# A hybrid decoder layer on one core: order in the head, one PSUM bank, one tie, tiles of their own, and the order of VectorE work in the down product

## The chip, the cores and the metric

The kernel runs on 1 core of one Trainium2 chip. Its time is device microseconds of that core; three runs of the kernel before gave 1724.09, 1722.09 and 1722.20 us, a median of 1722.2 us. The engines are called as in the profile: PE is TensorE (matmuls, and PEld its weight loads), DVE is VectorE, ACT is ScalarE, POOL is GpSimd, SP is the queue that issues the DMAs.

## What is computed

One decoder layer over 16 meta tokens and 1024 real tokens, all in float32. The reference, cut to its stages:

```
xn   = rms_norm(h, mix_pre_g)
proj = xn @ w_in                  # columns z, xbc (x, B, C), dt, q, k, v
y_ssd = ssd_mixer(z, silu(causal_dwconv(xbc)), softplus(dt + bias), ...)   # chunks of 128, a scan over chunks
y_sb  = rms_norm(stick_breaking_attention(q, k, v), sb_norm_g)             # 16 heads of 64
h = h + rms_norm(concat[y_ssd, y_sb] @ w_out, mix_post_g)
xn = rms_norm(h, ffn_pre_g)
gu = xn @ w_up                    # 1024 x 5632
g  = causal_dwconv3(gu[:, :2816])
f  = (gelu(g) * gu[:, 2816:]) @ w_down
h  = h + rms_norm(f, ffn_post_g)
```

## The kernel before

**Products.** Every large float32 product is made of three matmuls on operands split into a high and a low part: high by high, high by low, low by high. The high part is a copy on ACT, the low part a subtraction on DVE or POOL that reads the operand and the high part. Up and down products go through seven Strassen-Winograd products each instead of eight.

**Who orders the instructions.** A planner orders each engine's instructions by its own estimate of the times, except inside blocks in which the order of the text is kept: the head (all engines), the attention (PE alone), and from the second tile of the last mixing projection to the end (PE, DVE, ACT, POOL). `tc.issue_after(i)` ties the instructions traced in its block behind instruction `i` on `i`'s engine. Semaphores are set by a tracker of which instruction reads and writes which part of which tile.

**Head (lines 231 to 348).** Nine row tiles i = 0 to 8 are normed (`norm`, DVE), turned by PE transposes (`turn_x`, L288) and split into `xs`. Into that loop go half chains of the projections of B and C: `project_steps(..., halves_=True)` yields after the first four of eight row blocks of 128, 12 matmuls each. `chains[0]` is B0 and `chains[1]` C0; their weights are split by `split_hi` (ACT) and `split_lo` (POOL, in two halves).

**`to_tokens` (lines 482 to 492)** turns B, C and x back to tokens in three parts, each through a bank of PSUM from `psum_tp`, of which there are two, and copies each part out on DVE.

**Attention (lines 1012 to 1085).** For a pair of heads p and a query tile i, `block_weights` makes the logits z, ACT makes two sigmoids of each chunk (`kp`, `bt`), DVE scans, POOL multiplies; two blocks later `block_turn` transposes `bt` (`tw`) into the same two PSUM buffers (`zz`) that z uses, and ACT copies the result out (`th`; the last such copy is `copied[0]`); `block_mix` is the product with v. In p = 6 and 7 the eight rows of the first half of W_out are brought in by `wout_steps` (lines 898 to 907), here called k0 to k7: a load into one of two buffers `wraw`, a scaled copy on ACT (L904), a subtraction on DVE (L905), which frees the buffer. `STAGE` says after which block how many rows have been traced: k4 after (6,6), k5 after (6,7), k6 after (7,0), k7 after (7,1). Only k4 is tied behind `copied[0]` (line 1060).

**FFN operands (lines 1157 to 1258).** `half_x` makes the operands b11, b21, b22, t1, t2, t3, t4, each as high and low. The high and low tiles of these are flat, 2176 numbers a partition (two of them 2056), and a stretch of 2056 at a fixed offset (`FOFF`, 0 to 48) is seen as 4 x 514. The unsplit ones xa to xd are tiles of 4 x 514. `turn_x2`, `split_x` and `split_b22` fill column ranges of them in pieces: `split_x("t1", 0, 258)` the first columns, `turn_x2(7)` and `turn_x2(8)` the next two lots of 128, `split_b22` columns 2 to 257 and then 0 and 1. `g0_first`, `u0.first_half` and so on are the first products (L1351); each half ends with a copy on ACT (L1357, L1360), and the next product adds to the same bank.

**Down product (lines 1640 to 1880).** 77 steps s of 12 matmuls, in groups of 11 (`DOWN`: n = 1, 2, 6, 5, 3, 7, 4), into banks A or B. In step s come, in this order: the matmuls of s; after the last step of n = 5 and n = 7 the bank's copies or sums out (`evac2`, L1757); loads; `split_step(s + 3)`: ACT high parts (L1670) and DVE low parts (L1671) into one of WB = 3 buffers whi and wlo, which step s has just freed; for n = 6 also a difference `t2` first (L1668); the weight sums of `W_SUMS[s]` (DVE, L1675); one entry of `todo`. The last three steps 74 to 76 are run bank by bank with the end of the layer between.

```
for k in range(NPR):
    for at, args in ((18 + k, ("b11", "b12", "b11", ALU.subtract)), (16 + 2 * k, ("b21", "b21", "b22", ALU.subtract)),
                     (37 + k, ("b12", "b22", "b12", ALU.subtract)), (41 + k, ("b21", "b21", "b11", ALU.add))):
        W_SUMS.setdefault(at, []).append((k, *args))
```

Of the kernel before, what the change touches and what calls it, by code (L numbers as in the profile page):

```python
# [9 lines left out]
F32 = mybir.dt.float32  # L10
F32R = mybir.dt.float32r
BF16 = mybir.dt.bfloat16
AF = mybir.ActivationFunctionType
ALU = mybir.AluOpType
# [43 lines left out]
def tile_layer(ctx: ExitStack, tc: tile.TileContext, x, meta, rows, parts,  # L58
# [115 lines left out]
    def run(steps, n=None):  # L174
        for _ in steps if n is None else zip(range(n), steps):
            pass
# [54 lines left out]
    with tc.tile_pool(name="pre", bufs=3, side="right") as pre, \  # L231
            tc.manual_schedule(engines={ET.PE, ET.Activation, ET.DVE, ET.Pool, ET.SP}):
        spans = [(0, NM)] + [(NM + i * P, P) for i in range(NT)]
        xts = []

        def load_x(i):
            xts.append(pre.tile([P, D], F32, tag="xt", name=f"xt{i}", bufs=9))
            nc.sync.dma_start(out=xts[i][:spans[i][1]], in_=meta if i == 0 else x[(i - 1) * P:i * P, :])

        def raw_of(name, src):  # L240
            raw = wp.tile([P, KB, P], F32, tag="wraw", name=f"wr_{name}")
            nc.sync.dma_start(out=raw, in_=src)
            return raw

        load_x(0)
        load_x(1)
        gpre = row_bcast(pre, 0, D, "gpre")
        load_x(2)
        load_x(3)
        load_x(4)  # L250
        raw_dt = wp.tile([P, KB, 16], F32, tag="wraw", name="wr_dt")
        nc.sync.dma_start(out=raw_dt, in_=w_dt)
        raws = {"B0": raw_of("B0", w_xbc[8])}
        for i in range(5, NT + 1):
            load_x(i)
        raws["C0"] = raw_of("C0", w_xbc[10])
        nc.sync.dma_start(out=pp, in_=parts)

        sums, roots, norms = {}, {}, {}

        def square(i):
            if i <= NT:
                nr = spans[i][1]
                junk = pre.tile([P, D], F32, tag="junk", name=f"junk{i}", bufs=2)
                sums[i] = pre.tile([P, 1], F32, tag="ss", name=f"ss{i}")
                nc.scalar.activation(junk[:nr], xts[i][:nr], AF.Square, scale=D ** -0.5, accum_out=sums[i][:nr])

        def root(i):
            if i <= NT:
                roots[i] = rstd_of(pre, sums[i][:spans[i][1]], 1, spans[i][1], f"pre{i}")  # L270

        def norm(i):
            if i <= NT:
                nr = spans[i][1]
                norms[i] = pre.tile([P, D], F32, tag="xn", name=f"xn{i}", bufs=2)
                nc.vector.scalar_tensor_tensor(norms[i][:nr], xts[i][:nr], roots[i][:nr], gpre[:nr],
                                               op0=ALU.mult, op1=ALU.mult)

        def turn_x(i):
            c0, nr = spans[i]  # L280
            tps = []
            for hf in range(2):
                tp = (psum_tp, psum_z, psum_sd)[(2 * i + hf) % 3](f"xtp{i}_{hf}")
                if (2 * i + hf) % 3:
                    tp = tp.rearrange("p (a b) -> p a b", b=P)
                for b in range(4):
                    k = 4 * hf + b
                    nc.tensor.transpose(tp[:, b, :nr], norms[i][:nr, k * P:(k + 1) * P], ident[:nr, :nr])  # L288
                base = max(a for a, _ in CH if a <= c0)
                h, l = (xs[base][:, j, 4 * hf:4 * hf + 4, c0 - base:c0 - base + nr] for j in range(2))  # L290
                tps.append((tp, h, l))
            for tp, h, _ in tps:
                nc.scalar.activation(h, tp[:, :, :nr], AF.Copy)
            for tp, h, l in tps:
                nc.vector.tensor_tensor(l, tp[:, :, :nr], h.bitcast(F32), op=ALU.subtract)

        ws = {}

        def split_hi(name):
            hi = wp.tile([P, KB, P], F32R, tag="whi", name=f"wh_{name}", bufs=WB)  # L300
            lo = wp.tile([P, KB, P], F32R, tag="wlo", name=f"wl_{name}", bufs=WB)
            nc.scalar.activation(hi, raws[name], AF.Copy)
            ws[name] = hi, lo

        def split_lo(name, part):
            ks = slice(4 * part, 4 * part + 4)
            nc.gpsimd.tensor_tensor(ws[name][1][:, ks], raws[name][:, ks], ws[name][0][:, ks].bitcast(F32),
                                    op=ALU.subtract)

        chains = []  # L310
        for i in range(3):
            square(i)
            root(i)
        norm(0)
        norm(1)
        for i in range(NT + 1):
            if i == 4:
                run(dt_chain, 1)
            if i not in (2, 3):
                norm(i + 2)  # L320
            turn_x(i)
            if i != 2:
                square(i + 2 if i == 3 else i + 3)
                root(i + 2 if i == 3 else i + 3)
            if i == 3:
                norm(4)
                norm(5)
            if i == 1:
                hl = wp.tile([P, KB, 32], F32R, tag="whi", name="wh_dt", bufs=WB)
                nc.scalar.activation(hl[:, :, 0:16], raw_dt, AF.Copy)  # L330
                nc.gpsimd.tensor_tensor(hl[:, :, 16:32], raw_dt, hl[:, :, 0:16].bitcast(F32), op=ALU.subtract)
                dt_chain = dt_steps(hl)
            if i in (3, 4):
                split_hi("B0" if i == 3 else "C0")
            if i in (3, 4, 5):
                split_lo("B0" if i < 4 else "C0", int(i == 5))
            if i == 3:
                square(6)
                root(6)
                split_lo("B0", 1)  # L340
            if i == 3:
                chains.append(conv_chain(8, "B0", ws["B0"], True))
            if i in (5, 6):
                run(chains[0][1], 1)
            if i == 6:
                chains.append(conv_chain(10, "C0", ws["C0"], True))
            if i in (7, 8):
                run(chains[1][1], 1)

    halves = (slice(0, 64), slice(64, 128))  # L350
    M0 = NM - 2
# [111 lines left out]
    with tc.tile_pool(name="ssd", bufs=1, side="right") as sp:  # L463
# [17 lines left out]

        def to_tokens(src, dst, nm):
            for part in range(3):
                tp = psum_tp(f"tt_{nm}_{part}")
                if part == 0:
                    nc.tensor.transpose(tp[:NM, 0, :], src[:, 0:NM], ident)
                    nc.vector.tensor_copy(dst[:NM, 0, :], tp[:NM, 0, :])
                else:
                    for b in range(4):
                        t = 4 * (part - 1) + b  # L490
                        nc.tensor.transpose(tp[:, b, :], src[:, NM + t * P:NM + (t + 1) * P], ident)
                    nc.vector.tensor_copy(dst[:, 1 + 4 * (part - 1):5 + 4 * (part - 1), :], tp)
# [522 lines left out]
    for p in range(8):  # L1015
        for i in range(NT):
# [40 lines left out]
                edge = edge_turn(p - 1)  # L1057
            for _ in range(2):
                if wsteps and len(wres) < min(8, 3 * left[0], STAGE.get((p, i), 0)):
                    with tc.issue_after(copied[0]) if (p, i) == (6, 6) else ExitStack():  # L1060
                        run(wsteps, 1)
            if wsteps and first is None and len(wres) == 8:
                run(wsteps)
# [94 lines left out]
    def half_x(pool, dt, name):  # L1158
        if dt is F32:
            return pool.tile([P, 4, HW], dt, name=name, tag=name)  # L1160
        n, o = (4 * HW, 0) if name in ("b22l", "t1l") else (HF, FOFF.get(name[:-1], 0))
        return pool.tile([P, n], dt, name=name, tag=name)[:, o:o + 4 * HW].rearrange("p (k c) -> p k c", c=HW)

    rt = {n: (half_x(bp, F32R, f"{n}h"), half_x(bp, F32R, f"{n}l")) for n in ("b11", "b21")}
    xa, xb, xc, xd = (half_x(qp, F32, n) for n in ("xa", "xb", "xc", "xd"))
# [494 lines left out]

    def split_step(s):
        n, a, b, p = steps2[s]
        hi = wp.tile([P, 2, 512], F32R, tag="whi", name=f"dh{s}", bufs=WB)
        lo = wp.tile([P, 2, 512], F32R, tag="wlo", name=f"dl{s}", bufs=WB)
        sub = nc.vector.tensor_tensor
        if n == 6:
            wd["t2", p] = db.tile([P, 512], F32, tag="t2", name=f"t2_{p}", bufs=2)
# [8 lines left out]

    W_SUMS = {}
    for k in range(NPR):
        for at, args in ((18 + k, ("b11", "b12", "b11", ALU.subtract)), (16 + 2 * k, ("b21", "b21", "b22", ALU.subtract)),
                         (37 + k, ("b12", "b22", "b12", ALU.subtract)), (41 + k, ("b21", "b21", "b11", ALU.add))):  # L1680
            W_SUMS.setdefault(at, []).append((k, *args))

    for i in range(2, NFF):
# [114 lines left out]
             + [(None, nm, p) for p in range(NPR) for nm in ("b22", "b12")])  # L1798
    last_u = probs[-1]
    n2 = len(steps2)  # L1800
    todo = []
    db, facc = None, {}
    for k in range(3):
# [3 lines left out]
    for s in range(n2):  # L1807
        n, a, b, p = steps2[s]
        if s > 2 and s < n2 - 3:
            down_mm(s, (3, 0, 1, 2))  # L1810
            if p == NPR - 1 and n in (5, 7):
                for t in (3, 0, 1, 2):
                    evac2(n, t, banks[BANK[n], t])
        elif s == n2 - 3:
            for act in todo:
                act()
# [24 lines left out]
                fetch_w(pool or db, (nm,), k)  # L1841
        if s + 4 < n2:
            fetch_a(s + 4)
        if s + 3 < n2:
            split_step(s + 3)
        for args in W_SUMS.get(s, ()):
            w_sum(*args)
# [80 lines left out]
```

## Time and profile before

| | |
|---|---|
| median of 3 runs | 1722.2 us |
| the profiled execution's own time | 1724.05 us |
| its span, first to last instruction | 1722.1 us |
| mean granted TensorE clock | 0.999 |
| busy: PE, DVE, ACT, POOL | 99%, 64%, 48%, 48% of the span |
| moved by DMA | 173.87 MB, 101 GB/s |

A row of the timeline gives the start in us from the span's start, the time taken, engine, line, operation, the tiles written and read, the shapes, and how many such instructions were put together; in brackets stands how long the engine sat idle before it and whose end released it. A row of the windows gives a stretch, its length, the busy time and count of each engine, the granted clock, the share of the DMA engines and GB/s. Matmuls overlap, so a matmul's pace is read from start to start.

### The profile page before, as it was taken

How to read it: one execution, taken by the hardware profiler on the slowest of the kernel's cores; microseconds unless marked ns; L12 is line 12 of the kernel's file. 1: busy time of each engine (PE TensorE's matmuls, PEld its weight loads, DVE VectorE, ACT ScalarE, POOL GpSimd, SP SyncE). 2: the span in 40 equal slices, each digit the busy share in tenths (PEclk: the TensorE clock that was granted, in tenths of full speed). 3: DMA queues.
4: the chain of work that ended last, by engine and by line, in shares of the span. 5: the costliest groups of instructions: out<-in, count | busy, mean ns of one | idle time of the engine just before them, and what ended most of it. 6: DMA issues, size and time to landing. Idle time of an engine off the chain costs nothing. (4 is left out here: it accounts for less than half of the span.)

```text
span 1722.1 us, 28048 instructions
## 1 busy us (share of the span) xinstructions
PE 1699.6 (99%) x11230; PEld 1495.4 (87%) x11230; DVE 1105.8 (64%) x1234; ACT 821.0 (48%) x1370; POOL 833.9 (48%) x641
## 2 busy tenths in 40 slices
PE   7999999999999999999999999999999999999998
PEld 6999889888989998998788788999988888887886
DVE  6752973875676677577530667675666666659777
ACT  5423663554566566557653344433333333344544
POOL 4323664585566575565552222587767777300001
PEclk9999999999999999999999999999999999999999
DMA  4232333231011111112214553233322223395345
GB/s 164 56 114 93 109 124 111 68 104 38 26 38 38 33 31 38 38 50 76 76 66 153 208 172 123 68 111 110 105 92 92 92 92 103 122 327 177 105 115 177
DMA packets 90674, 173.87 MB, mean 101 GB/s; under 512 B 10704, under 2 KB 35816, under 8 KB 90544
## 3 DMA queue, kind: packets, MB, share of 16 engines
q1 hardware_dynamic: 90544, 172.08, 31.3%
q8 instruction: 88, 1.44, 0.3%
q14 instruction: 42, 0.34, 0.1%
HBM read 122.32 MB, written 49.73 MB: 100 GB/s over the span
## 5 line engine op out<-in xcount | busy, mean ns | idle before, releaser
L792 POOL TENSOR_TENSOR bt<-bt,kp 128x256 f32<-128x256 f32 (+7 forms) x128 | 212.0, 1675 | 184.5 <-DVE kp L790 143.6
L790 DVE TENSOR_TENSOR_SCAN kp<-kp,hold 128x272 f32<-128x272 f32 (+7 forms) x128 | 183.4, 1473 | 24.6 <-ACT kp L783 14.3
L1287 POOL TENSOR_TENSOR wlo<-wr,whi 128x1024 fp32r<-128x1024 f32 x43 | 99.3, 2318 | 42.7 <-ACT whi L1286 42.7
L1785 POOL TENSOR_TENSOR fms<-fms 128x1 f32<-128x1 f32 x8 | 2.9, 362 | 223.7 <-ACT dh L1670 197.0
L783 ACT ACTIVATE kp<-z 128x288 f32<-128x288 f32 (+6 forms) x112 | 82.7, 739 | 50.8 <-PE z L782 25.8
L1286 ACT ACTIVATE whi<-wr 128x1024 fp32r<-128x1024 f32 x43 | 45.7, 1064 | 111.2 <-PE fX L1337 67.5
L169 PE MATMUL pj_v<-xs,wh_v 128*128 128x400 f32 (+2 forms) x384 | 95.0, 334 | 0.0
L169 PE MATMUL pj_k<-xs,wh_k 128*128 128x400 f32 (+2 forms) x384 | 94.6, 333 | 0.0
L169 PE MATMUL pj_q<-xs,wh_q 128*128 128x386 f32 (+2 forms) x384 | 93.9, 331 | 0.0
L806 ACT ACTIVATE th<-tw 128x1024 f32<-128x1024 f32 (+2 forms) x96 | 75.5, 815 | 37.5 <-PE tw L804 37.3
L1670 ACT ACTIVATE dh<-ar 128x512 fp32r<-128x512 f32 x77 | 48.5, 630 | 93.2 <-PE dnB L1748 44.7
L169 PE MATMUL pj_X<-xs,wh_X 128*128 128x400 f32 (+2 forms) x384 | 92.0, 327 | 0.0
L169 PE MATMUL pj_z<-xs,wh_z 128*128 128x386 f32 (+2 forms) x384 | 91.6, 326 | 0.0
L1409 DVE SCALAR_TENSOR_TENSOR ga<-gr,pp,ga 128x1024 f32<-128x1024 f32 x44 | 69.0, 1567 | 34.4 <-ACT ga L1402 33.6
L758 DVE CAST qh<-q 128x128 fp32r<-128x128 f32 x64 | 46.5, 727 | 69.1 <-PE z L782 68.7
L976 PE MATMUL mo<-woa,yh 128*128 128x512 f32 x256 | 85.5, 400 | 0.0
L1671 DVE TENSOR_TENSOR dl<-ar,dh 128x512 fp32r<-128x512 f32 x77 | 53.2, 691 | 50.2 <-ACT dh L1670 50.1
L784 ACT ACTIVATE bt<-z 128x288 f32<-128x288 f32 (+6 forms) x112 | 83.1, 742 | 0.0
L804 PE MATMUL tw<-ident,bt 128*128 128x128 f32 x576 | 75.7, 274 | 2.2 <-POOL cb L793 1.7
L819 PE MATMUL av<-th,v 128*64 128x128 f32 x1152 | 77.2, 278 | 0.0
L819 PEld LDWEIGHTS av<-th,v 128*64 128x64 f32 x1152 | 61.6, 137 | 13.8 <-issue 10.9
L804 PEld LDWEIGHTS tw<-ident,bt 128*128 128x128 f32 x576 | 65.4, 141 | 8.7 <-issue 3.1
(560 smaller groups left out, 5603.9 us busy)
## 6 DMA issues: line engine op xcount, KB each, us to landing
wr<-in_w_up SPq DMA_DIRECT2D x44, 512.0 KB
fds<-ga SPq DMA_DIRECT2D x44, 256.0 KB
b<-in_w_down SPq DMA_DIRECT2D x44, 256.0 KB
ar<-fds SPq DMA_DIRECT2D x44, 256.0 KB
fda<-ga SPq DMA_DIRECT2D x33, 256.0 KB
ar<-fda SPq DMA_DIRECT2D x33, 256.0 KB
yk<-yd SPq DMA_DIRECT2D x16, 512.0 KB
wor<-in_w_out SPq DMA_DIRECT2D x12, 512.0 KB
```

The source lines that it names most:

```text
L169: mm(acc[:ncol, :n - s], a[:, k, :ncol], xs[c0][:, b, k, s:n], start=(k == 0 and j == 0), stop=(k == KB - 1 and j == 2))
L783: nc.scalar.activation(kp[:, :, a:a + w], z[:, :, :w], AF.Sigmoid, scale=-QSCALE)
L784: nc.scalar.activation(bt[:, :, a:a + w], z[:, :, :w], AF.Sigmoid, scale=QSCALE)
L790: nc.vector.tensor_tensor_scan(kp[:, j][:, ::-1], kp[:, j][:, ::-1], hold[:, L - n:L][:, ::-1], 0.0, op0=ALU.mult, op1=ALU.max)
L792: nc.gpsimd.tensor_tensor(bt[:, j, 0:m], bt[:, j, 0:m], kp[:, j, 1:m + 1], op=ALU.mult)
L804: nc.tensor.transpose(tw[:, j, b, :], bt[:, j, c0:c0 + P], ident)
L806: copied[0] = nc.scalar.activation(th[:, :, :nb, :], tw[:, :, :nb, :], AF.Copy).ins
L819: mm(av[halves[j], :], v[:, kb, halves[j]], th[:, j, b, :], start=kb == 0, stop=kb == i)
L976: recent[0] = mm(acc, u[:, k, :], v[:, cs], start=(k == 0 and j == 0), stop=(k == 7 and j == 2))
L1287: nc.gpsimd.tensor_tensor(l, raw, h.bitcast(F32), op=ALU.subtract)
L1409: nc.vector.scalar_tensor_tensor(v, self.g[jj][:, :, i:i + 256], fconv_w[:, j, i:i + 1], v, op0=ALU.mult, op1=ALU.add)
L1671: sub(lo[:, k], raw, hi[:, k].bitcast(F32), op=ALU.subtract)
```

## The change

1. Head: the half chains of B0 move from the end of turns i = 5 and 6 to a place before `turn_x(i)` of the same i; those of C0 likewise for i = 7 and 8. C0's chain is opened at i = 7 instead of at the end of i = 6.
2. `to_tokens`: part 0 of B1 goes through a bank of `psum_z` instead of `psum_tp`.
3. W_out's row k5, traced at (6,7), is tied behind `copied[0]` as k4 is.
4. `half_x`: the stretch of 4 x 514 becomes a tile of that shape; what stood ahead of it and behind it in the flat tile becomes two tiles that nothing uses.
5. Down: the sums b21 - b22 of k = 2 to 10 move from steps 20, 22 ... 36 to steps 34 to 42; the sums b21 + b11 from steps 41 to 51 to steps 44 to 54; the split of step 67 is issued in step 65 behind the `evac2` of n = 7 instead of in step 64; the split of the last step, 76, gets buffers of its own.

```
@@ head, in the loop over i
             if i not in (2, 3):
                 norm(i + 2)
+            if i in (5, 6):
+                run(chains[0][1], 1)
+            if i == 7:
+                chains.append(conv_chain(10, "C0", ws["C0"], True))
+            if i in (7, 8):
+                run(chains[1][1], 1)
             turn_x(i)
...
             if i == 3:
                 chains.append(conv_chain(8, "B0", ws["B0"], True))
-            if i in (5, 6):
-                run(chains[0][1], 1)
-            if i == 6:
-                chains.append(conv_chain(10, "C0", ws["C0"], True))
-            if i in (7, 8):
-                run(chains[1][1], 1)
@@ to_tokens
-                tp = psum_tp(f"tt_{nm}_{part}")
+                if part == 0 and nm == "B1":
+                    tp = psum_z(f"tt_{nm}_{part}").rearrange("p (a b) -> p a b", b=P)
+                else:
+                    tp = psum_tp(f"tt_{nm}_{part}")
@@ rows of W_out
-                    with tc.issue_after(copied[0]) if (p, i) == (6, 6) else ExitStack():
+                    with tc.issue_after(copied[0]) if (p, i) in ((6, 6), (6, 7)) else ExitStack():
                         run(wsteps, 1)
@@ half_x
         n, o = (4 * HW, 0) if name in ("b22l", "t1l") else (HF, FOFF.get(name[:-1], 0))
-        return pool.tile([P, n], dt, name=name, tag=name)[:, o:o + 4 * HW].rearrange("p (k c) -> p k c", c=HW)
+        if o:
+            pool.tile([P, o], F32, name=f"{name}o", tag=f"{name}o")
+        t = pool.tile([P, 4, HW], dt, name=name, tag=name)
+        if n > o + 4 * HW:
+            pool.tile([P, n - o - 4 * HW], F32, name=f"{name}e", tag=f"{name}e")
+        return t
@@ split_step
-        hi = wp.tile([P, 2, 512], F32R, tag="whi", name=f"dh{s}", bufs=WB)
-        lo = wp.tile([P, 2, 512], F32R, tag="wlo", name=f"dl{s}", bufs=WB)
+        own = s == len(steps2) - 1
+        hi, lo = ((db if own else wp).tile([P, 2, 512], F32R, tag=f"w{e}" + "l" * own, name=f"d{e[0]}{s}",
+                                           bufs=1 if own else WB) for e in ("hi", "lo"))
@@ W_SUMS
-(16 + 2 * k, ("b21", "b21", "b22", ALU.subtract))
+(16 + 2 * k if k < 2 else 32 + k, ("b21", "b21", "b22", ALU.subtract))
-(41 + k, ("b21", "b21", "b11", ALU.add))
+(44 + k, ("b21", "b21", "b11", ALU.add))
@@ the loop over s
+    LATE = 6 * NPR - 2
...
                 for t in (3, 0, 1, 2):
                     evac2(n, t, banks[BANK[n], t])
+            if s == LATE + 1:
+                split_step(LATE + 3)
...
-        if s + 3 < n2:
+        if s + 3 < n2 and s != LATE:
             split_step(s + 3)
```

More of the change, by code (lines that the diff above doesn't have):

```diff
@@ L1678, in tile_layer @@
     for k in range(NPR):
-        for at, args in ((18 + k, ("b11", "b12", "b11", ALU.subtract)), (16 + 2 * k, ("b21", "b21", "b22", ALU.subtract)),
-                         (37 + k, ("b12", "b22", "b12", ALU.subtract)), (41 + k, ("b21", "b21", "b11", ALU.add))):
+        for at, args in ((18 + k, ("b11", "b12", "b11", ALU.subtract)), (16 + 2 * k if k < 2 else 32 + k, ("b21", "b21", "b22", ALU.subtract)),
+                         (37 + k, ("b12", "b22", "b12", ALU.subtract)), (44 + k, ("b21", "b21", "b11", ALU.add))):
             W_SUMS.setdefault(at, []).append((k, *args))
```

## The prediction

> **What bounds the kernel now.** I read the page first, then a table of stretches, then PE's timeline at each place where PE stands still.
>
> ```profile
> span 1722.1 us, 28048 instructions
> PE 1699.6 (99%) x11230; PEld 1495.4 (87%) x11230; DVE 1105.8 (64%) x1234; ACT 821.0 (48%) x1370; POOL 833.9 (48%) x641
> ```
> ```profile
> 800.00:815.00 15.00, 12.78 (x124) 11.16 (x123) 12.92 (x10) 12.93 (x20) 8.61 (x4) 1.00 0.23 71
> 1060.00:1080.00 20.00, 17.91 (x113) 16.14 (x112) 13.99 (x18) 8.50 (x16) 2.71 (x4) 0.91 0.34 106
> 1500.00:1700.00 200.00, 199.97 (x875) 163.24 (x874) 149.82 (x239) 95.59 (x177) 5.39 (x8) 1.00 0.60 192
> ```
>
> PE is the bound: 1722.1 - 1699.6 = 22.5 us of it are idle, and the change removes no matmul. It can gain only where PE idles, where PE is busy at less than its pace, or where the clock is down; it can lose where it opens a new gap. The table has 2.2 us idle at 800 to 815, 2.1 us at 1060 to 1080 with the clock at 0.91, and none in the down product from 1500, where lost time has to be looked for in the pace.
>
> **The change part by part**
>
> **1. Head.**
>
> ```profile
> 20.99 1.06 PE L288 MATMUL xtp<-ident,xn 128*128 128x128 f32 x8 [1.15 <-DVE xn L276]
> 24.08 1.04 PE L288 MATMUL xtp<-ident,xn 128*128 128x128 f32 x8
> 27.15 1.04 PE L288 MATMUL xtp<-ident,xn 128*128 128x128 f32 x8
> ```
> ```profile
> 17.74 2.02 POOL L307 TENSOR_TENSOR wl_B<-wr_B,wh_B 128x512 fp32r<-128x512 f32 x1
> 21.54 1.29 POOL L307 TENSOR_TENSOR wl_B<-wr_B,wh_B 128x512 fp32r<-128x512 f32 x1
> 24.61 1.29 POOL L307 TENSOR_TENSOR wl_C<-wr_C,wh_C 128x512 fp32r<-128x512 f32 x1
> ```
>
> PE waits 1.15 us for turn 5's normed rows, with B0's first half chain behind it. That chain's low weights are there at 17.74 + 2.02 = 19.76, when PE falls idle (20.99 - 1.15 = 19.84). A turn and a half chain take 27.15 - 24.08 = 3.07 us, so a half chain about 2.0 to 2.3. Ahead of turn 5 it fills the gap and turn 5 begins near 22.1. The second half chain then comes near 23.1 (weights at 22.83), C0's first near 26.2 (weights at 25.90). The margins are 0.1 to 0.3 us. Gain 1.15; with a weight late by its margin 0.8, and no less than 0, since all that is late here was late before.
>
> **2. B1's first part.**
>
> ```profile
> 310.92 0.66 PE L491 MATMUL tt_B<-ident,bt 128*128 128x128 f32 x4 [0.48 <-DVE bn L487]
> ```
>
> Part 2 waits for a bank that part 0 still holds; with part 0 in another bank it does not. Gain 0.48. If the scan's first product wanted that bank next it would be 0.
>
> **3. Row k5.**
>
> ```profile
> 804.62 1.15 ACT L904 ACTIVATE woa<-wor,pp 128x1024 fp32r<-128x1024 f32 x1 [1.99 <-DMA wor<-in_w_out]
> 807.69 0.93 ACT L784 ACTIVATE bt<-z 128x912 f32<-128x912 f32 x1
> 811.45 1.21 ACT L904 ACTIVATE woa<-wor,pp 128x1024 fp32r<-128x1024 f32 x1
> ```
> ```profile
> 808.72 1.06 PE L804 MATMUL tw<-ident,bt 128*128 128x128 f32 x8 [1.69 <-POOL cb L793]
> 810.32 0.44 PE L804 MATMUL tw<-ident,bt 128*128 128x128 f32 x2 [0.53 <-ACT bt L784]
> 838.07 0.48 PE L976 MATMUL mo<-woa,yh 128*128 128x512 f32 x1
> ```
> ```profile
> 829.28 1.28 DVE L905 SCALAR_TENSOR_TENSOR woa<-wor,pp,woa 128x1024 fp32r<-128x1024 f32 x1
> ```
>
> The row at 804.62 cannot be k4, which is tied behind the copies out of this block's transposes (PE begins them at 808.72); k4 is the one at 811.45. So the planner put k5 ahead of k4, and ACT, in order, stood 1.99 us for k5's load and 1.15 us on it with the sigmoids queued behind. The first pair ends at 807.69 + 0.93 = 808.62, and at 808.72 the transposes get that buffer; POOL's product is named, but the end that fits is ACT's. With k5 tied at (6,7), ACT does the sigmoids some 3.1 us earlier, more than the 1.69 + 0.53 = 2.22 that PE idles. Gain 2.22.
>
> What is late next: k5 frees its buffer a block later, so k7's load is issued later; behind it in SP's queue stand the loads of y. PE wants rows k4 to k7 at 838.07, and the last of them was ready at 829.28 + 1.28 = 830.56, so 7.5 us are there, against a block of about 7 to 8 us less what k6 may do first. Bounds: the 2.22 in full, or the same idle anew where ACT waits for another row's load (0), or 1.99 once more on top (-2).
>
> **4. FFN operands.**
>
> ```profile
> 1065.75 0.21 ACT L1248 ACTIVATE b22h<-b22e 128x8 fp32r<-128x8 f32 x1 [4.73 <-DVE b22l L1249]
> 1070.94 0.63 ACT L1242 ACTIVATE t1h<-xa 128x512 fp32r<-128x512 f32 x1 [2.01 <-DVE t1l L1243]
> 1071.47 0.58 ACT L1357 ACTIVATE gr<-g0a 128x516 f32<-128x516 f32 x1
> 1077.16 1.08 ACT L1224 ACTIVATE xb<-x2tp 128x512 f32<-128x512 f32 x2
> ```
> ```profile
> 1068.48 1.29 DVE L1194 SCALAR_TENSOR_TENSOR oxn<-mb,rs_ff,gffn 128x1024 f32<-128x1024 f32 x1 [1.31 <-POOL rs_ff L196]
> 1078.39 0.68 DVE L1226 TENSOR_TENSOR xb<-x2tp,xb 128x512 f32<-128x512 f32 x1
> ```
> ```profile
> 1069.91 1.06 PE L1200 MATMUL x2tp<-ident,oxn 128*128 128x128 f32 x8 [0.96 <-DVE oxn L1194]
> 1072.11 0.58 PE L1351 MATMUL g0a<-b21h,whi2g 128*128 128x258 f32 x1 [1.14 <-ACT gr L1357]
> ```
> ```profile
> 1072.10:1075.20 3.10, 3.09 (x14) 3.09 (x15) 2.17 (x4) 1.56 (x3) 0.00 (x0) 0.50 0.17 67
> ```
>
> Both ACT waits are for DVE to finish reading columns that ACT does not write: columns 0 and 1 of b22h against 2 to 257, a later 128 of t1h against its first 258. In the tiles of 4 x 514 this does not happen: ACT writes xb for turn 7 and turn 8 in one go at 1077.16 while DVE reads turn 7's part only at 1078.39. So I take it that the tracker sees a flat tile's column stretches as one run, and that tiles of that shape lose both waits. Then b22h's edge comes 4.7 us earlier, and turn 8's normed rows (1068.48) wait only for their row sum, some 1.7 us earlier, which covers PE's 0.96; and the copy `gr` (1071.47) no longer stands behind the 2.01 us wait, which covers the 1.14. What PE needs next, t1's last part, moves up with turn 8.
>
> The clock stands at 0.50 for the 3.10 us right behind these gaps: 1.55 us of work lost. With the idle gone I take it as gone. Gain 0.96 + 1.14 + 1.55 = 3.65; bounds 0 (the waits stay) and 3.65. [...]
>
> **5. Down.**
>
> ```profile
> 1533.51 29.92 PE dnB L1748 x132
> 1563.42 22.28 PE dnA L1748 x96
> 1585.71 9.34 PE dnA L1748 x36
> ```
> ```profile
> 1569.01 1.29 DVE L1675 TENSOR_TENSOR b<-b,b 128x512 f32<-128x512 f32 x2
> 1684.01 2.48 DVE L1757 TENSOR_TENSOR facc<-dnA,facc 128x512 f32<-128x512 f32 x4
> ```
> ```profile
> 1684.42 0.39 PE L1748 MATMUL dnA<-dl,dh 128*128 128x512 f32 x1
> 1684.84 0.47 PE L1748 MATMUL dnA<-dh 128*128 128x512 f32 x1
> ```
> ```profile
> 1706.92 0.63 ACT L1670 ACTIVATE dh<-ar 128x512 fp32r<-128x512 f32 x1 [0.95 <-PE dnA L1748]
> ```
> ```profile
> 1707.86 0.39 PE L1748 MATMUL dnA<-dl,dh 128*128 128x512 f32 x1
> 1709.27 0.39 PE L1748 MATMUL dnA<-dh 128*128 128x512 f32 x1
> ```
>
> The pace is 29.92 / 132 = 0.227 us, 2.72 a step. The 132 matmuls of n = 6 take 1595.05 - 1563.42 = 31.63, so 1.71 are lost while PE looks busy. DVE is why: a step there has a difference, two low parts and a sum, 4 x 0.62 = 2.5 us, and 3.1 with a second sum or a bank's sum. In turn over 11 steps: four bank sums and some six second sums are 10 x 0.62 = 6.2 us over a slack of 11 x 0.2 plus the two to three microseconds by which splits run ahead. Without the second sums 2.5 us stay over, which that covers: gain 1.71. The sums land in steps of n = 5 and 3, where there is no difference to make: at most 4 x 0.62 = 2.5 of 2.72. If they did not fit, about 0.2 a step over nine steps would come back, 1.8.
>
> At 1684.42 the pace breaks by 0.42 - 0.23 = 0.19, because the four bank sums wait on DVE behind the split of step 67; moved ahead of it, that and the 0.13 in the next step go: 0.32. The split of 67 is then done near 1687, just as PE comes to it. At 1706.92 the last split has waited for step 73 to free its buffer; four matmuls take 1.41 instead of 0.91. With its own buffer it starts about 1 us earlier: gain 0.50. Bounds of both: 0 and 0.8. Together 2.53.
>
> **Sum.** 1.15 + 0.48 + 2.22 + 3.65 + 2.53 = 10.03 us. The profiled execution took 1724.05 in all (its span 1722.1 and 1.95 around it): 1714.0. It is 1.85 over the median; the runs of before lie at 1722.1, 1722.2 and 1724.1, as if some did without the half-clock stretch. From the median without that term, 1722.2 - 8.5 = 1713.7. I take **1714.0**.
>
> **The rivals**
>
> **A, ACT waits for another row.** With k4 and k5 tied, k6 is the first free row, and the planner may put it ahead as it put k5; its load can start only when k4 is done. For it: the 1.99 us at 804.62 shows that the planner thinks loads quicker than they are. Against it: k6 has a block more before anyone is short of it. Term 3 becomes 0 to -2: 1716.2 to 1718.2, say 1717.0.
>
> **B, the waits at 1065 and 1070 stay**, because the tracker does not go by the tile's shape: term 4 is 0, 1717.7. Against it stands xb.
>
> [...]
>
> **D, slower.** The new unused tiles shift the operands, and PE reads them at another pace throughout the FFN.
>
> ```profile
> L1337 PE MATMUL fA<-b11h,whi 128*128 128x258 f32 (+1 forms) x120 | 38.4, 320 | 0.0
> L1337 PE MATMUL fX<-t2h,whi 128*128 128x258 f32 (+1 forms) x120 | 38.2, 318 | 0.0
> ```
>
> The stage is some 440 us of pure PE (1060 to 1500). Against it: b11 at offset 0 and t2 at offset 40 read alike, 320 and 318 ns. It decides from 10 / 440 = 2.3% of pace, and at 4% gives 1714 + 17.6 = 1731.6.
>
> **How the numbers follow.** Forecast 0.62; A 0.17; B 0.07; C 0.08; D 0.03; 0.03 for a planner's order that gives back 5 us or more. The forecast's own spread is 1712.5 to 1715.5. With A to C the range is 1711.5 to 1718.5. What a measurement of this kernel can tell from no change is about 0.2%, 3.4 us: faster means under 1718.8. The forecast, C, B and nearly all of A are that: 0.91. Same: 0.05. Slower: 0.04.
>
> **What would show it.** Head: no idle before turn 5. B1: no wait of `tt_B` for `bn`. W_out: all eight rows on ACT in order, the fifth and sixth behind the copies of (6,6) and (6,7), no idle of PE on `tw`; wrong if ACT waits for a `wor` load with sigmoids behind it. FFN: no wait of ACT for b22l or t1l, clock 1.00 from 1060 to 1080. Down: 29.92 us for n = 6's 132 matmuls, no break at the first matmul of step 66 or in the last three steps. The prediction is wrong if PE shows a gap over 1 us anywhere new.

## The result, and the profile after

| | before | after |
|---|---|---|
| median of 22 runs each | 1724.18 us (1721.37 to 1726.51) | 1721.65 us (1718.95 to 1725.26) |
| ratio after / before, 95% interval | | 0.9986 (0.998 to 0.9992) |
| the profiled execution's own time, its span | 1724.05, 1722.1 us | 1721.23, 1719.2 us |

Three executions that ran far slower (5874, 2783 and 4233 us, one each of no_tie, both_mended and ffn_only below) are left out of every median and ratio in this document.

The kernel became 2.5 us faster, where 10 were forecast and 5.7 were the least that the range allowed. The page of the kernel after, its first lines (busy time, share of the span, instructions):

```profile
span 1719.2 us, 28051 instructions
PE 1698.1 (99%) x11230; PEld 1496.7 (87%) x11230; DVE 1108.8 (64%) x1234; ACT 822.4 (48%) x1370; POOL 834.4 (49%) x641
```

PE still idles 21.1 us, 1.4 less than before. Its waits after (engine, line, what released it; total us, times, longest):

```profile
PE av L822 <- ACT th L809: 2.3, 1, 2.3
PE sg L637 <- ACT sgh L628: 1.9, 2, 1.4
PE z L785 <- ACT th L809: 0.9, 1, 0.9
```

None of these three was there before; the waits at turn 5, on `tt_B`, on `tw` and at 1069 to 1072 are gone. (The lines of the changed kernel stand 3 later than before from `to_tokens` on, 8 from `half_x` on, 9 in the down product.) The windows after, by stage (stretch, its length, busy us and count of PE, PEld, DVE, ACT, POOL, granted clock, DMA share, GB/s):

```profile
300.00:330.00 30.00, 28.12 (x171) 24.89 (x170) 19.78 (x28) 13.76 (x32) 8.83 (x6) 0.89 0.12 36
...
800.00:845.00 45.00, 41.73 (x393) 33.38 (x393) 37.35 (x34) 32.95 (x51) 30.04 (x22) 1.00 0.24 73
1060.00:1080.00 20.00, 20.00 (x145) 18.57 (x144) 17.67 (x22) 12.54 (x21) 4.95 (x5) 1.00 0.34 106
```

Two of these stretches before:

```profile
300.00:330.00 30.00, 29.52 (x191) 26.39 (x190) 23.01 (x31) 16.66 (x41) 13.56 (x7) 1.00 0.15 42
800.00:845.00 45.00, 42.65 (x395) 31.49 (x394) 34.75 (x34) 30.46 (x48) 27.19 (x19) 1.00 0.26 79
```

1060 to 1080 is as forecast: no idle, clock 1.00. New is 300 to 330: 1.4 us less of PE than before, and a clock of 0.89. From 800 to 845 PE has 0.9 us less. Where the time went is read from the starts of the same PE instructions in both traces:

| PE instruction | before | after | after lies | since the row above |
|---|---|---|---|---|
| B1's first transpose `tt_B` | 309.56 | 308.06 | 1.50 ahead | gained 1.50 |
| the scan's first `yt` of group 1 | 325.64 | 328.87 | 3.23 behind | lost 4.73 |
| first `z` after 834 | 835.34 | 839.14 | 3.80 behind | lost 0.57 |
| first matmul of down | 1503.42 | 1503.28 | 0.14 ahead | gained 3.94 |
| last matmul of down | 1715.20 | 1712.61 | 2.59 ahead | gained 2.45 |

The remaining 0.3 to the spans' 2.9 lies in the tail. So head, FFN operands and down gave 7.9 us where the forecast had 1.15 + 3.65 + 2.53 = 7.33. B1's first part lost 4.7 where it was to gain 0.48, and the row of W_out lost 0.57 where it was to gain 2.22.

**The loss at 308 to 329.** In the scan over chunks PE's product `sg` reads a high part `sgh`, eight copies on ACT, and a low part `sgl`, one product on POOL. `ct` is C after its convolution: sums on DVE, then a silu on ACT. `yt` is a chunk's result, turned on PE. The timeline of the kernel after, DVE, POOL, ACT and PE (the row at 313.80 is the last of the three sums that the row above it holds together):

```profile
312.75 3.19 DVE L478 SCALAR_TENSOR_TENSOR ct<-craw_C,pp,ct 128x256 f32<-128x256 f32 x3
...
313.80 2.15 DVE L478 SCALAR_TENSOR_TENSOR ct<-craw_C,pp,ct 128x256 f32<-128x256 f32 x1
...
313.76 1.90 POOL L630 TENSOR_TENSOR sgl<-tri,adl 128x1024 fp32r<-128x1024 f32 x1 [1.19 <-PE sg L637]
...
315.98 0.42 ACT L480 ACTIVATE ct<-ct 128x256 f32<-128x256 f32 x1 [4.78 <-DVE ct L478]
316.30 0.48 ACT L391 ACTIVATE q<-pj_q 128x386 f32<-128x386 f32 x1
316.80 1.28 ACT L639 ACT_TABLE_LOAD   x1
...
319.63 0.50 PE L637 MATMUL sg<-sgh,lowr 128*128 128x512 f32 x1 [1.44 <-ACT sgh L628]
...
320.80 0.61 PE L637 MATMUL sg<-sgh,lowr 128*128 128x512 f32 x1 [0.43 <-ACT sgh L628]
```

The same place before:

```profile
314.26 1.52 DVE L478 SCALAR_TENSOR_TENSOR ct<-craw_C,pp,ct 128x256 f32<-128x256 f32 x3
...
315.96 1.90 POOL L627 TENSOR_TENSOR sgl<-tri,adl 128x1024 fp32r<-128x1024 f32 x1 [1.89 <-PE sg L634]
...
316.65 1.23 DVE L440 COPY meta_q<-q 64x2 f32<-64x2 f32 x1 [0.86 <-ACT q L391]
```

POOL's product `sgl` starts when PE has used the `sgl` of the chunk before. Before, that was at 315.96, when DVE's three sums of `ct` had ended (314.26 + 1.52 = 315.78). After, PE reaches that place 0.7 us sooner against DVE, since it no longer stands at `tt_B`; the third sum comes at 313.80, 0.04 us behind POOL, and takes 2.15 us: it ends at 315.95, just behind POOL's 313.76 + 1.90 = 315.66. The three take 3.19 us instead of 1.52. The silu of `ct`, the copy of `q`, the table load and then the eight `sgh` stand behind it on ACT in that order, and PE waits 1.44 + 0.43 us for `sgh`. (Before, the copy `meta_q` ran into POOL's product in the same way: 1.23 us, ending at 317.88 with POOL's 317.86, where the next copy of that size takes 0.17. PE waited for nothing there.) On top comes the clock, windows after:

```profile
317.63:321.04 3.41, 1.53 (x7) 0.78 (x6) 0.65 (x3) 3.40 (x13) 0.00 (x0) 1.00 0.00 0
321.04:324.46 3.42, 3.42 (x7) 1.49 (x7) 2.05 (x2) 3.14 (x11) 1.90 (x1) 0.50 0.02 5
324.46:327.87 3.41, 3.41 (x17) 3.41 (x18) 1.70 (x3) 0.34 (x2) 1.42 (x1) 0.50 0.00 0
```

Half clock for 6.83 us is up to 3.41 of work. 1.87 + 3.41 = 5.28, less the 0.72 gained at `tt_B` (0.48 idle and 0.24 of a broken pace), is 4.6, against 4.73 measured from `tt_B` to `yt`.

**The loss at 800 to 845.** ACT of the kernel after:

```profile
822.55 1.15 ACT L907 ACTIVATE woa<-wor,pp 128x1024 fp32r<-128x1024 f32 x1 [2.18 <-DMA wor<-in_w_out]
823.60 0.58 ACT L809 ACTIVATE th<-tw 128x512 f32<-128x512 f32 x1
824.08 1.14 ACT L907 ACTIVATE woa<-wor,pp 128x1024 fp32r<-128x1024 f32 x1
...
834.45 1.15 ACT L907 ACTIVATE woa<-wor,pp 128x1024 fp32r<-128x1024 f32 x1 [2.40 <-DMA wor<-in_w_out]
...
837.12 1.06 ACT L964 ACTIVATE yh<-yk 128x1024 fp32r<-128x1024 f32 x1 [1.36 <-DMA yk<-yd]
838.08 1.92 ACT L809 ACTIVATE th<-tw 128x1024 f32<-128x1024 f32 x2
```

In ACT's order the row at 822.55 is k6 and the one at 824.08 is k5: with k5 tied, the planner put k6's copy ahead of it, and k6's load had begun only when k4 had freed its buffer (818.29). The copy `th` that PE wants stands behind: 2.34 us. k7 takes k5's buffer, which DVE freed at 830.78; its load lands at 834.45, and behind it wait the load of `yk` in SP's queue, then `yh` and `th` on ACT: 0.86 us more of PE. So 3.20 us of waits came for the 2.22 that went; in the starts it is 0.57. The buffers come free late also because DVE's subtractions of k4 and k5 (815.53 and 827.69) took 2.74 and 3.09 us, begun while POOL was on a product `bt`, where that of k6 (831.20), with POOL idle, took 1.28; before it was the same (2.73, 3.09 and 1.28).

### The profile page after: what moved, and what is told of

Its sections match the earlier page's. It is cut to its first block, busy times and chain, and to the rows that moved or that the text cites. A ratio compares the mean times of both kernels' runs of the same rounds, so it can differ in the third digit from the quotient of the medians.

```text
span 1719.2 us, 28051 instructions
## 1 busy us (share of the span) xinstructions
PE 1698.1 (99%) x11230; PEld 1496.7 (87%) x11230; DVE 1108.8 (64%) x1234; ACT 822.4 (48%) x1370; POOL 834.4 (49%) x641
## 3 DMA queue, kind: packets, MB, share of 16 engines
q8 instruction: 88, 1.44, 0.3%
## 4 chain that ended last, share of the span: by engine, by line
PE 51%; DVE 0%; DVEq 0%; POOLq 0%; ACT 0%; issue 0%; POOL 0%; ACTq 0%
PE mo L979 10%; PE fX L1345 10%; PE dnA L1757 7%; PE fA L1345 7%; PE fY L1345 7%; PE dnB L1757 5%; PE g0a L1359 1%; PE av L822 1%; PE tw L807 0%; PE x2tp L1208 0%; PE z L785 0%; PE g0c L1359 0%; PE g0d L1359 0%; PE u0a L1359 0%; PE u0d L1359 0%; PE u0c L1359 0%
```

## The experiments

The kernels named by part hold the parts of the change by their numbers above. Each was timed beside the kernel before, in three groups (by its median: 1724.83, 1725.51, 1723.55); across groups the ratios compare better than the medians.

| kernel | median us | before beside it | ratio, 95% interval |
|---|---|---|---|
| no_bank (1, 3, 4, 5) | 1717.86 | 1724.83 | 0.9966 (0.9954 to 0.9978) |
| no_tie (1, 2, 4, 5) | 1721.76 | 1724.83 | 0.9983 (0.9974 to 0.9992) |
| neither (1, 4, 5) | 1716.90 | 1724.83 | 0.9963 (0.9951 to 0.9975) |
| both_mended | 1717.58 | 1724.83 | 0.9963 (0.995 to 0.9976) |
| sgl_dve | 1717.51 | 1725.51 | 0.9957 (0.9942 to 0.9973) |
| k4_free | 1715.92 | 1725.51 | 0.995 (0.9938 to 0.9963) |
| bank_only (2) | 1726.45 | 1725.51 | 1.0014 (1.0004 to 1.0023) |
| ffn_only (4) | 1721.21 | 1725.51 | 0.9978 (0.9968 to 0.9988) |
| head_only (1) | 1723.14 | 1723.55 | 0.9997 (0.9988 to 1.0006) |
| down_only (5) | 1722.06 | 1723.55 | 0.9989 (0.9979 to 0.9998) |
| ffn_again (4) | 1720.51 | 1723.55 | 0.9978 (0.9969 to 0.9987) |
| all_mended | 1717.21 | 1723.55 | 0.9967 (0.9954 to 0.998) |

**no_bank**: the changed kernel without part 2.

```
-                if part == 0 and nm == "B1":
-                    tp = psum_z(f"tt_{nm}_{part}").rearrange("p (a b) -> p a b", b=P)
-                else:
-                    tp = psum_tp(f"tt_{nm}_{part}")
+                tp = psum_tp(f"tt_{nm}_{part}")
```

> All parts of the change but part 2 (B1's first part through psum_tp again). Theory, a collision of POOL with DVE: without PE's 0.72 us at the second transpose group (0.48 idle and a broken pace) POOL's sgl starts 0.7 us sooner against DVE and falls on DVE's three sums of ct (3.19 us instead of 1.52); so with part 2 undone the three sums take 1.5 us, PE waits for no sgh at the start of group 1's scan (1.44 and 0.43 in the changed kernel), and the 0.48 us at tt_B is back. With the half clock at 321 to 328 a consequence of these waits, the profiled run is near 1721.2 - 1.9 - 3.4 + 0.7 = 1716.6. Rival, the earlier head or another part moved the planner or the loads: sg still waits 1.9 us, 1721.9. Rival for the clock, the half stretch is not the waits': it stays without them, 1720.0.

Its windows, as above:

```profile
300.00:330.00 30.00, 29.52 (x191) 26.40 (x190) 22.99 (x31) 17.40 (x43) 13.56 (x8) 1.00 0.17 45
800.00:845.00 45.00, 42.59 (x389) 32.43 (x386) 35.55 (x33) 30.21 (x47) 28.25 (x19) 0.96 0.25 79
```

300 to 330 is again as before the change, in PE and in clock; the median is 3.8 us under the changed kernel's. One part of 0.48 us carried the whole loss there. At 800 to 845 the wait on k6's load is still there (2.41 us of PE at 820), and now the clock falls behind it.

**no_tie** and **neither**: without part 3, and without parts 2 and 3.

```
-                    with tc.issue_after(copied[0]) if (p, i) in ((6, 6), (6, 7)) else ExitStack():
+                    with tc.issue_after(copied[0]) if (p, i) == (6, 6) else ExitStack():
```

> All parts of the change but part 3 (k5 tied at (6,7)). Theory, ACT waits for the loads of k6 and k7 because k5's late copy frees its buffer late and k6's copy stands ahead of k5's: the waits of ACT at 822 and 834 and PE's 2.34 and 0.86 us are gone, the 1.69 and 0.53 us on tw at (6,6) are back; 1721.2 - 3.2 + 2.2 = 1720.2. Rival, the waits come from the earlier head, not from the tie: 2.34 and 0.86 stay, 1723.4.

> Parts 1, 4 and 5 alone (head, FFN operands, down). Theory: no wait on sgh, no half clock at 321, the old waits of 0.48 on tt_B and 2.2 on tw: 1716.6 - 1.0 = 1715.6. If the half clock stays, about 1719.

In no_tie PE waits 1.88 us on `tw` and neither 2.34 nor 0.86 on `th`, as expected; on `sgh` it still waits 1.9. The median, 1721.76, doesn't differ from the changed kernel's 1721.65. In neither the waits are 0.53 + 0.53 on `tw` and 0.47 on `tt_B`, and 1716.9 is 4.86 under no_tie, which has the bank, and 0.96 under no_bank, which has the tie. So the bank costs 3.8 us (changed against no_bank) to 4.9 in the medians, 3.4 by the ratios. What the tie costs isn't shown: 0.96 us lies within the intervals of no_bank and neither, and with the bank there is no difference.

**both_mended**: all five parts, with `sgl` of one chunk on DVE, and k4 and k5 both traced at (6,6) behind the same copy.

```
-            nc.gpsimd.tensor_tensor(sgl[:nr, :, :nr], tri[...
+            (nc.vector if (g, c) == (1, 1) else nc.gpsimd).tensor_tensor(sgl[:nr, :, :nr], tri[...
-    STAGE = {..., (6, 6): 5, (6, 7): 6, ...}
+    STAGE = {..., (6, 6): 6, (6, 7): 6, ...}
-                    with tc.issue_after(copied[0]) if (p, i) in ((6, 6), (6, 7)) else ExitStack():
+                    with tc.issue_after(copied[0]) if (p, i) == (6, 6) else ExitStack():
```

> The changed kernel with both losses taken away: sgl of group 1's chunk 1 on DVE instead of POOL, and W_out's k5 traced with k4 at (6,6), both behind the same copy (no tie at (6,7)). Theory: DVE's sums of ct take 1.5 us, PE waits neither for sgh nor for th nor for tw, no half clock: 1721.2 - 1.9 - 3.4 - 3.2 = 1712.7. Rival, the PE waits are those of a changed order and not of POOL beside DVE: sg waits 1 us or more still, 1717 or above.

The first half held: PE waits 0.43 us for `sgh`, the clock is 1.00 to the end. The second did not: ACT waits 0.80 and 1.22 us for k6 and k7, whose buffers DVE frees only at 813.5 and 816.2, and PE loses 1.13 and 0.85. 1717.58, and the profiled execution's 1716.42, miss the 1712.7.

**sgl_dve**: the changed kernel with that one instruction on DVE alone.

> The changed kernel, all five parts, with sgl of group 1's chunk 1 on DVE instead of POOL; only this instruction moves. Theory, POOL beside DVE: DVE's three sums of ct take 1.5 us again (3.19 in the changed kernel) although B1's first part still goes through the scan's bank, and of PE's 1.44 + 0.43 us on sgh at most 0.43 stay; no half clock at 321; median near 1721.65 - 1.4 - 2 to 3 = 1717.5 to 1718.2, as without part 2. Rival, the bank itself is late (sg waits for a buffer that B1's first part holds): the wait stays 1.9 us and the median 1721.6.

Its DVE and ACT, and the wait of PE that is left at the scan:

```profile
313.52 1.53 DVE L478 SCALAR_TENSOR_TENSOR ct<-craw_C,pp,ct 128x256 f32<-128x256 f32 x3
...
316.07 1.20 DVE L630 TENSOR_TENSOR sgl<-tri,adl 128x1024 fp32r<-128x1024 f32 x1
...
315.08 0.42 ACT L480 ACTIVATE ct<-ct 128x256 f32<-128x256 f32 x1 [3.12 <-DVE ct L478]
...
319.90 0.50 PE L637 MATMUL sg<-sgh,lowr 128*128 128x512 f32 x1 [0.43 <-ACT sgh L628]
```

B1's first part still goes through the scan's bank, the sums take 1.53 us, of the two waits 0.43 is left, and 4.1 us are back (1717.51). The rival, a bank that comes free late, falls: the bank is the same, only POOL's work is gone. But the bank gains nothing even so: from `tt_B` to the first `yt` of group 1 this trace takes 16.08 us (308.82 to 324.90), as before (309.56 to 325.64), where the changed kernel takes 20.81. PE comes 0.7 us sooner and then waits, for `sgh`: the sums of `ct` and ACT set the time there, and they start no sooner.

**bank_only**: the kernel before with part 2 alone.

> The kernel before with part 2 alone. Theory: tt_B's 0.48 us goes, PE waits 1.4 + 0.4 us on sgh, the clock is halved behind it when both waits fall in one window of 3.41 us; 1724.5 - 0.7 + 1.9 + 1.7 to 3.4 = 1727.4 to 1729.1, slower than before. Rival, the loss needs the earlier head: no wait on sgh, 1724.0.

Its DVE and POOL:

```profile
315.04 3.19 DVE L478 SCALAR_TENSOR_TENSOR ct<-craw_C,pp,ct 128x256 f32<-128x256 f32 x3
...
316.05 1.90 POOL L630 TENSOR_TENSOR sgl<-tri,adl 128x1024 fp32r<-128x1024 f32 x1 [1.20 <-PE sg L637]
```

and two of its windows:

```profile
318.62:322.03 3.41, 1.98 (x12) 1.66 (x11) 1.44 (x8) 3.38 (x10) 0.00 (x0) 1.00 0.00 0
322.03:325.45 3.42, 2.99 (x11) 1.58 (x12) 1.27 (x2) 3.42 (x11) 1.50 (x1) 1.00 0.02 5
```

3.19 us again, with the old head: the loss needs no other part, and this edit alone makes the kernel slower (1.0014). In the profiled execution the clock did not fall, with the two waits in two windows, and `tt_B` to `yt` is 17.72 us, 1.64 more than before. The median, 1726.45, lies under the expected 1727.4.

**ffn_only**, **head_only**, **down_only**, **ffn_again**: the kernel before with the hunks of one part each, as shown in the change. ffn_again is ffn_only once more, and its trace is the one read.

> The kernel before with part 4 alone. Forecast of part 4: the waits of 0.96 and 1.14 us at 1070 and 1072 and the half clock behind them go: 1724.5 - 3.65 = 1720.9, and the other gaps stay. Rival, the half clock is a matter of where the windows fall and not of these waits: 1722.4, and a half stretch elsewhere.

> The kernel before with part 1 alone. Forecast: the 1.15 us ahead of turn 5 go and at most 0.45 us come in their place (B0's chain waiting for wl_B); PE waits for no sgh at group 1's scan, since its order there is as before; the gaps at 810 and 1070 stay. 1725.0 - 0.7 to 1.15 = 1724.0. Rival, the head's shift alone already brings the wait on sgh: 1726 or above.

> The kernel before with part 5 alone. Forecast: all seven groups of 132 matmuls take 29.9 us, 2.5 us less in all; 1725.0 - 2.5 = 1722.5. Rival, the sums fall late where they were moved to: 0.8 us, 1724.2.

> The kernel before with part 4 alone, once more for its trace. Forecast: no wait of ACT for b22l or t1l, no idle of PE and a clock of 1.00 from 1060 to 1080, the waits at 21, 311 and 810 as before; 1721.5. Rival: the waits of 0.96 and 1.14 us stay, 1725.

In ffn_again PE is busy 20.00 of 20.00 us from 1060 to 1080 at a clock of 1.00; the medians of the two give 4.3 and 3.0 us, against 3.65. In down_only all groups of 132 matmuls but the last, whose three closing steps are run by banks, take 29.92 or 29.93 us; down's first to last matmul takes 209.29 us against 211.78 before, 2.5 less; the medians give 1.5. In head_only the 1.15 us are gone and 0.38 stand in their place, where B0's chain waits for its low weights; 0.4 us in the medians is within what can be told from none.

**k4_free**: parts 1, 4 and 5, with k4 not tied, and k5 traced at (6,6) and tied there. **all_mended**: all five parts, with this and with `sgl` on DVE.

```
-    STAGE = {..., (6, 6): 5, (6, 7): 6, ...}
+    STAGE = {..., (6, 6): 6, (6, 7): 6, ...}
-                    with tc.issue_after(copied[0]) if (p, i) == (6, 6) else ExitStack():
+                    with tc.issue_after(copied[0]) if (p, i) == (6, 6) and len(wres) == 5 else ExitStack():
```

> Parts 1, 4 and 5, with another order of W_out's rows: k4 not tied, k5 traced at (6,6) too and tied behind copied[0]. Theory, a copy on ACT must come after its load and must free its buffer a load's time (4.8 us) ahead of the next: k4, loaded long before, is copied near 800 without a wait, k6's load starts near 803, k5 is copied behind the copies near 808, k7's load starts near 814: no wait of ACT for a wor load, none of PE on tw or th from 800 to 840. Against parts 1, 4 and 5 alone that is 1.06 us: 1716.9 - 1.1 = 1715.8. Rival, DVE frees the buffers late whatever ACT does: ACT waits 0.5 to 1.2 us for k6 or k7 and the median stays 1716.9.

> All five parts of the change with both losses mended: sgl of group 1's chunk 1 on DVE, k4 not tied, k5 traced at (6,6) and tied behind copied[0]. Theory: of the changed kernel's new waits 0.43 us on sgh and at most 1.25 us on tw are left, no idle of 1.7 us falls into one window of the clock: 1715.9 as without B1's first part in the scan's bank, less its 0.7, plus 0.4: 1715.6. Rival, DVE's extra instruction makes something else late: 1717 or above.

The `-` lines are those of the kernel before. k4_free has the lowest median of the study, 1715.92 us, 0.5% under before and 5.7 us under the changed kernel. The expected 1715.8 was met without its mechanism: k4 and k6 are copied without a wait, but k7's load is late by 1.62 us on ACT, and PE idles 1.25 us on `tw`, where in neither it idles 1.06. So nothing shows this order of rows to be better than that of neither (1716.9); the intervals overlap. all_mended, at 1717.21, shows no gain on it, and from `tt_B` to `yt` it takes 16.08 us as sgl_dve does: B1's first part through another bank brings nothing, with `sgl` on DVE either.

## Why the prediction was wrong

**1, head: the mechanism right, the size of one draw.** There is no idle at turn 5, and PE is 1.50 us ahead at `tt_B`; 0.17 of it was there at the first turn (8.47 before, 8.30 after). The gap that went is not the same in every execution: in the four traces with the old head it is 1.15, 0.99, 1.98 and 1.15 us (before, bank_only, down_only, ffn_again). In four of the nine with the new one a weight is late, by 0.38 to 0.45 us, more than the margin of 0.1 to 0.3. The medians of head_only can't tell this part from nothing.

**2, B1's first part: the step that failed.** The working went from the wait to the bank, asked who wants that bank next, and gave 0.48 with 0 as its lower end. That took PE's wait to be on the path of the scan, which sgl_dve shows it wasn't (16.08 us with the wait and without), and it never asked what PE's earlier arrival sets free. That was POOL's `sgl`, and the two rows that decide it were in the trace of before, 0.18 us apart: DVE's sums ended at 315.78, POOL began at 315.96, on PE's signal. Taking 0.72 us out of PE alone turned the order round. In place of +0.48 the runs show -3.4 to -4.9 (no_tie against neither, changed against no_bank, by ratios and medians), and -0.9 to -2.4 alone (bank_only: medians and ratio).

**3, row k5: rival A's mechanism, at a price in its range.** The forecast reckoned only who needs k4 to k7 last (838) and found 7.5 us. What counts is where ACT meets each copy: k6 was put ahead of k5, before its load. So the 2.22 were not gained: the trace lost 0.57. That the tie itself costs anything is not shown: from the `yt` to the `z` of the table of starts the three traces with the tie as changed take 510.3 to 510.9 us, the seven with k5 untied 508.7 to 511.3. The term itself was also read from one draw: with k5 untied, PE's idle on `tw` came out at 2.22, 1.06, 1.88, 1.06, 2.78, 0.92 and 2.44 us in the seven profiles (before, neither, no_tie, bank_only, head_only, down_only, ffn_again), which goes with ACT's wait for k5's load: 1.99 us before, 0.82 in neither, 2.73 in ffn_again. What makes that load late or early stays open.

**4, FFN operands: right, with some luck in the size.** Both waits of ACT went, PE's 0.96 + 1.14 and the half stretch with them: 3.94 from `z` to down in the trace. So the waits hung on how these tiles are declared, as the prediction took it, and rival B fell. So did C, the 0.08 for a half stretch that stays when these gaps go: after, the clock is 1.00 from 1060 to 1080. But the 1.55 us of the half stretch are not in every execution: of the four traces that keep these gaps, before and down_only have a clock of 0.91 from 1060 to 1080, bank_only and head_only 1.00.

**5, down: right, 2.45 for 2.53.** From the chain of the kernel after that ended last, the groups of n = 2 and n = 6:

```profile
1533.41 29.92 PE dnB L1757 x132
1563.33 29.92 PE dnA L1757 x132
```

31.63 became 29.92, and no step from 65 on is long any more. Rival D fell: the matmuls `fA` on b11h take 320 ns and `fX` on t2h 318 in the mean, as before.

**The sum.** With terms 2 and 3 as the trace has them, 1.50 - 4.73 - 0.57 + 3.94 + 2.45 + 0.3 = 2.9 us, the difference of the spans. Left to a planner's order that gives back 5 us or more was 0.03; the planner's order there changed by one matmul, only who came first changed, and no case was kept for that. Two of the prediction's own signs of being wrong came up: ACT waited for a `wor` load with sigmoids behind it (822.55), and PE has new gaps over 1 us (1.44 and 2.34). The 2.5 us that were left are also less than the 3.4 that the prediction took as the least it could tell, an outcome it gave 0.05.

## What to carry to other kernels

Where a wait is taken off an engine, list what that engine's next instructions release, and lay the starts of those beside what runs then: an arrival 0.7 us earlier can be worth less than nothing when it lets a long instruction of POOL in ahead of one of DVE that is on the path (here a product of 1.90 us, 0.04 us ahead; 3.8 us lost by the medians). Ask first whether the engine that waits is on the path there at all: a wait taken off it may only come back at its next one. A tie that makes a copy later makes its buffer's next load later too, and the planner may put that next copy ahead of the tied one. A wait for a load is priced from several executions, and an idle of PE of some 1.8 us or more within 3.41 us has to be priced with the clock behind it, which stood at 0.50 here for the next 3.41 us or for two such stretches.

## What the runs showed of the hardware

**A sum on DVE behind a product on POOL.** A DVE sum of two operands that came 0.03 or 0.04 us behind a product on POOL ended 0.3 us after it and took 2.14 or 2.15 us in place of some 0.5, in all three traces with that order (the changed kernel, no_tie, bank_only: 3.18 or 3.19 us for the three sums). With POOL's product 0.18 us behind the last sum (before) the three took 1.52 us, with the product on DVE (sgl_dve) 1.53. Why DVE takes longer there is not shown; the runs show it in this order of the two only.

**Half clock behind some 1.8 us of idle.** Up to PE's last matmul the half stretches last 3.41 us (before, 1071.82 to 1075.24), at 321 in the changed kernel (321.04 to 327.87) and at 322 in no_tie twice that. A clock of 0.50 begins again behind PE's last matmul, before at 1720.35, 190 steps of 3.413 us after 1071.82, and in the changed kernel at 1717.08, 409 such steps after 321.04. So the windows below are counted in steps of 3.413 us from an edge of a half stretch in the same trace; the second row of a fence is the window behind the first. Before, a window without a half stretch behind it, and the one ahead of its half stretch at 1071.82:

```profile
805.59:809.00 3.41, 1.72 (x15) 1.54 (x15) 3.20 (x2) 3.41 (x6) 2.65 (x2) 1.00 0.00 0
...
1068.41:1071.82 3.41, 1.60 (x11) 0.97 (x9) 3.25 (x4) 1.40 (x3) 0.03 (x1) 1.00 0.31 64
```

no_bank, behind the wait on k6's load:

```profile
817.69:821.10 3.41, 1.00 (x16) 0.59 (x11) 3.41 (x2) 2.45 (x3) 1.18 (x1) 1.00 0.01 4
821.10:824.52 3.42, 3.42 (x18) 3.42 (x18) 3.42 (x4) 2.29 (x6) 3.42 (x2) 0.50 0.00 0
```

down_only, at the FFN gaps:

```profile
1070.44:1073.85 3.41, 1.61 (x12) 1.41 (x13) 2.95 (x4) 1.72 (x4) 0.00 (x0) 1.00 0.45 136
1073.85:1077.27 3.42, 3.42 (x18) 3.42 (x17) 1.98 (x3) 1.00 (x2) 0.00 (x0) 0.50 0.05 18
```

head_only, at `tw`:

```profile
804.69:808.10 3.41, 1.75 (x16) 1.49 (x12) 2.33 (x2) 3.41 (x5) 2.96 (x3) 1.00 0.00 0
808.10:811.52 3.42, 2.30 (x19) 2.10 (x20) 3.07 (x5) 3.42 (x7) 0.00 (x0) 1.00 0.50 153
```

With PE busy 0.98 (ffn_again) to 1.60 us of a window (the changed kernel's 1.53 among them) the clock was halved in the next, with 1.72, 1.75 and 1.98 (bank_only) it was not; with 1.61 it was in down_only and was not in all_mended. So the bound in these traces is about 1.8 us of idle, pieces added up, and a gap of that size costs up to 1.7 us, half of 3.41 (3.4 at 321), or nothing by where it falls. That is one reason why runs of one kernel lie 1 to 7 us apart: of the changed kernel's, the one with a mean granted clock of 0.999 took 1719.69 us, the two with 0.995 took 1724.63 and 1725.26. Why the stretch at 321 lasted two windows stays open: PE was busy throughout the first (3.42 of 3.42 us).

**Half clock behind a window without a gap.** In neither, PE's timeline

```profile
871.42 1.94 PE L877 MATMUL avm<-wcm,meta_v 16*128 16x4 f32 x16
```

and two windows:

```profile
871.55:874.96 3.41, 3.41 (x32) 3.02 (x34) 0.34 (x2) 0.87 (x2) 3.41 (x4) 1.00 0.00 0
874.96:878.37 3.41, 3.41 (x21) 2.69 (x18) 1.39 (x1) 2.91 (x5) 0.58 (x4) 0.50 0.50 156
```

PE has no gap in the first window, yet the clock is halved behind it: 1.82 us of it are these sixteen matmuls, which move 4 columns each. They stand at the same place in every kernel here. In the six traces where 1.82 (neither) to 1.94 us (no_tie, next window at 0.50) of them fell into one window, the next was at half clock; in the seven where the larger share in one window was 1.03 to 1.79 us (the changed kernel, next window at 1.00), it was not. So the clock behaves as if such matmuls counted like idle, up to the same bound; no kernel here changes them to test it.
